# A written hand-over with the next weights cast earlier, and another order of the seven block products

## The chip, the cores and the metric

The kernel runs on one core of a Trainium2 chip. The core has a matrix engine (TensorE, PE in the rows; its weight loads are PEld), a vector engine (VectorE, DVE), a scalar engine (ScalarE, ACT), GpSimd (POOL) and a queue engine that issues transfers (SyncE, SP). Each engine works through its own list of instructions in order and waits where an operand or a buffer is not there yet. The metric is the device time of one execution in microseconds, the median of three runs.

## The reference

Two layers act on a sequence of 512 tokens with 1024 channels, all in float32. Each layer has three sublayers, each between two RMS norms and added to the residual `x`:

```
h = rms_norm(x, norm_pre[l, 0])
x = x + 0.5 * rms_norm(swiglu_ffn(h, ...ffn1...), norm_post[l, 0])
h = rms_norm(x, norm_pre[l, 1])
x = x + rms_norm(hybrid_mixer(h, ...), norm_post[l, 1])
h = rms_norm(x, norm_pre[l, 2])
x = x + 0.5 * rms_norm(swiglu_ffn(h, ...ffn2...), norm_post[l, 2])

def swiglu_ffn(h, w_gate, w_up, w_down):
    return (silu(h @ w_gate) * (h @ w_up)) @ w_down      # 1024 -> 2816 -> 1024
```

The mixer projects h into the inputs of three branches (stick-breaking attention, a gated convolution, gated linear attention), gates and sums them, and ends in an output projection of 1024 x 1024.

## The kernel before

**Products.** A float32 value is split into two parts, hi (a cast by ACT) and lo (the difference, by DVE), and each product is three matmuls: hi by hi, hi by lo and lo by hi. Every weight tile therefore costs a load into a `raw` buffer (half of one of three), one ACT cast `whi` and one DVE subtraction `wlo`. `whi` and `wlo` have five buffers each; a buffer is free again when the last matmul that reads it is done.

**Tokens.** The 512 tokens are four tiles of 128, numbered 0 to 3 (a, b, c, d in `out_proj`). A sublayer ends in `out_proj`: the last four weight tiles (`TAIL`) are kept back and multiplied token by token (`token(i)`), so that token 0's result is complete first. Token 3 goes tile by tile instead, so that each weight buffer comes free after six matmuls.

**Hand-over.** A `Hand` object per token holds what lies between the result and the next sublayer: `sum` (the block products of the FFN added up; nothing after a mixer), `square` (ACT, with a sum along the row), `mean` (one small DVE operation and a power on POOL), `scaled` (tn, the result by the post norm's weight), `add` (the new residual x, two DVE operations, and its two squares on ACT) and `normal` (hn, two DVE operations). `arrival(i, hns, forms)` transposes a token's hn on PE (eight transposes, tile pt), splits it into xh and xl, and, where the next sublayer is an FFN, hands it to `Forms.arrive`, which copies it to `xr` on ACT for tokens 0 and 1 and forms T1 to T4 on DVE for tokens 2 and 3. The copies are traced behind the split of the same PSUM banks.

The next sublayer's first weights are made by a generator `steps` of four steps, one `load_w` each: for an FFN two steps of the gate's and two of the up projection's first 256 columns, for a mixer four steps of two rows of blocks of V. The next stage's first matmuls are called pf (FFN; all eight k of the gate, then token i+1 arrives, then the up projection) or pv (mixer; token i+1 arrives after four of eight k). `second` is called at token 1's place there and ends token 3's hand-over.

**What fixes the order.** `pinned` chains an instruction behind the one that was traced just before it on the same engine. With `held[0]` true, the casts of `split` are pinned as well; else the planner of the framework may move them. All matmuls are pinned.

**Down projection.** `Down` multiplies 16 of the 22 row blocks as a 2 x 2 block product with seven products (`ORDER`: name, weight blocks, bank pair). Each has `PER` = 4 steps, and a step is twelve matmuls of 512 columns. Two of the other row blocks (`MIDDLE`) and four (`LAST`) are multiplied plainly; a middle step has 24 matmuls. `sums` loads the weights of a step and forms their sum (one DVE operation of 128 x 1024 for S3, S2, S1 and A22, none for A11, A12 and S4; S2 also adds two tiles of the hidden values first); S3 loads two blocks a step, the others one. `parts` makes the casts: dh and whi on ACT, dl and wlo on DVE. In A12 it also adds two tiles of the hidden values for S4. `ahead` runs `sums` of one step and `parts` of the step before it; it is called three times at the end of the block products of gate and up (`block_tiles`) and is four steps ahead of the matmuls (`AHEAD`). `tap` copies a bank pair to SBUF between products.

Of the kernel before, what the change touches and what calls it, by code (L numbers as in the profile page):

```python
# [41 lines left out]
def kernel(  # L42
# [184 lines left out]
    def arrival(i, hns, forms):  # L227

        t = slice(i * P, (i + 1) * P)
        if i == 0:  # L230
            room("xh")
            room("xl")
        pts = []
        for j, hn in enumerate(hns):
            pt = bank("pt")
            for k in range(4):
                transpose(pt[:, k * P:(k + 1) * P], hn[:, k * P:(k + 1) * P], ident)
            src = pt.rearrange("p (k t) -> p k t", t=P)
            split(cur["xh"][:, 4 * j:4 * j + 4, t], cur["xl"][:, 4 * j:4 * j + 4, t], src)
            pts.append(src)  # L240
        if forms is not None:
            forms.arrive(i, pts)
# [58 lines left out]
    def out_proj(w2d, nk, stat, tail, finish, upcoming, early, head=None):  # L301


        ld = lambda k: load_rows(w2d, k)
        fresh = head is None
        if fresh:
            banks = [[bank(f"o{i}{h}", "pb" if i < 3 else "pa") for h in range(2)] for i in range(NT)]
        else:
            banks, rest = head

        def mms(i, h, k, sh, sl, wh, wl):
            mm_out(banks[i][h], slice(i * P, (i + 1) * P), sh, sl, wh[:, HS[h]], wl[:, HS[h]],
                   fresh and k == 0, k == nk - 1)

        for k in range(nk - tail if fresh else 0):
            wh, wl = ld(k)
            sh, sl = stat(k)
            for i in range(NT):
                for h in range(2):
                    mms(i, h, k, sh, sl, wh, wl)  # L320
        if fresh:
            rest = [(k, ld(k), stat(k)) for k in range(nk - tail, nk)]
        def token(i):
            for h in range(2):
                for k, (wh, wl), (sh, sl) in rest:
                    mms(i, h, k, sh, sl, wh, wl)

        if early is None:
            for i in range(NT):
                token(i)  # L330
                finish(i, banks[i])
            return None

        held[0] = True
        a, b, c, d = [finish(i, banks[i]) for i in range(NT)]
        forms = finish(None, None)
        w, steps = early()
        next(steps)
        token(0)
        a.half(0)  # L340
        a.half(1)
        a.mean()
        token(1)
        a.add()
        b.half(0)
        a.mean()
        b.sum(1)
        a.normal()
        b.square(1)
        b.scaled(1)  # L350
        b.mean()
        token(2)
        c.half(0)
        b.add()
        c.half(1)
        b.mean()
        c.mean()
        b.normal()
        arrival(0, a.hns, forms)

        for k, (wh, wl), (sh, sl) in rest:
            for h in range(2):
                mms(NT - 1, h, k, sh, sl, wh, wl)
        c.add()
        next(steps)
        c.mean()
        d.sum(0)
        d.sum(1)
        d.square(0)
        d.square(1)  # L370
        next(steps)
        d.scaled(0)
        d.scaled(1)
        for _ in steps:
            pass
        d.mean()
        c.normal()
        held[0] = False

        def second():  # L380
            arrival(1, b.hns, forms)
            d.add()
            d.mean()
            d.normal()

        upcoming.extend((None, second, lambda: arrival(2, c.hns, forms), lambda: arrival(3, d.hns, forms)))
        return w

# [179 lines left out]
    class Down:  # L568
# [1 line left out]
        R1, R2 = slice(256, 512), slice(0, 256)  # L570
        PER = NP // 2

        ORDER = (("A11", ((0, 0),), "A"), ("S3", ((0, 1), (1, 1)), "C"), ("S2", ((0, 0),), "A"),
                 ("A12", ((1, 0),), "B"), ("S1", ((1, 1),), "A"), ("S4", ((1, 1),), "A"), ("A22", ((1, 0),), "C"))
        AHEAD = 4
        MIDDLE, LAST = (0, 1), (18, 19, 20, 21)

# [22 lines left out]

        def plan(self):

            self.steps = [(j, c) for j in range(5) for c in range(self.PER)]
            self.steps += [(None, f) for f in self.MIDDLE]
            self.steps += [(j, c) for j in (5, 6) for c in range(self.PER)]
            self.end = len(self.steps)
            self.steps += [(None, f) for f in self.LAST]

# [24 lines left out]
        def sums(self, p):  # L633

            self.load(p)
            j, c = self.steps[p]
            if j is None:
                return
            name, raws = self.ORDER[j][0], self.raw[p]
            tt = lambda o, a, b, op: pinned(nc.vector.tensor_tensor(o, a, b, op=op))  # L640
            kept = None if j == 0 else self.kept[:, 2 * c:2 * c + 2, :].rearrange("p k c -> p (k c)")
            src = raws[0]
            if name == "S3":
                tt(kept, raws[0], raws[1], ALU.subtract)
                src = kept
            if name == "S2":
                for q, x in enumerate(self.of(p)):
                    tt(x, self.s1[c][:, q], x, ALU.add)
                tt(kept, kept, raws[0], ALU.subtract)
                src = kept  # L650
            if name == "S1":
                pinned(nc.vector.scalar_tensor_tensor(src, kept, -1.0, raws[0], op0=ALU.mult, op1=ALU.subtract))
            if name == "A22":
                tt(src, kept, raws[0], ALU.add)
            self.raw[p] = src

        def parts(self, p):

            j, c = self.steps[p]
            sh, sl = (slot(x, F32R, "s") for x in ("dh", "dl"))  # L660
            hi, lo = (wp.tile([P, 1024], F32R, tag=t, name=t) for t in ("whi", "wlo"))
            of, src = self.of(p), self.raw.pop(p)
            n = 512 // len(of)
            cut = [slice(q * n, (q + 1) * n) for q in range(len(of))]
            for q, x in zip(cut, of):
                pinned(nc.scalar.copy(sh[:, q], x))
            pinned(nc.scalar.copy(hi, src))  # L667
            for q, x in zip(cut, of):
                pinned(nc.vector.tensor_tensor(sl[:, q], x, sh[:, q].bitcast(F32), op=ALU.subtract))
            pinned(nc.vector.tensor_tensor(lo, src, hi.bitcast(F32), op=ALU.subtract))  # L670
            if j is not None and self.ORDER[j][0] == "A12":
                for q, x in enumerate(of):
                    pinned(nc.vector.tensor_tensor(x, x, self.hid[self.F0 + 2 * c + q][:, self.R1], op=ALU.add))
            self.ready[p] = sh, sl, hi, lo

        def ahead(self):
# [10 lines left out]
        def product(self, p):  # L687
            j, c = self.steps[p]
            sh, sl, hi, lo = self.ready.pop(p)
            if j is None:  # L690
                for i, h in ((0, 1), (1, 1), (0, 0), (1, 0), (2, 0), (3, 0), (2, 1), (3, 1)):
                    mm_out(self.out[i][h], slice(i * P, (i + 1) * P), sh, sl, hi[:, HS[h]], lo[:, HS[h]],
                           st=(c == self.MIDDLE[0] and i < 2 and h == 1))
                return
            b = self.banks[self.ORDER[j][2]]
            for q in range(2):
                w = slice(q * 512, (q + 1) * 512)
                for i in range(2):
                    t = slice(q * 256 + i * P, q * 256 + (i + 1) * P)
                    mm_out(b[i], t, sh, sl, hi[:, w], lo[:, w], st=(q == 0 and c == 0 and j in (0, 1, 3)))  # L700

        def run(self, late):
            c0, d0, c1, d1, b0, b1 = (bank(n) for n in ("oC", "oD", "oC", "oD", "oB", "oB"))
# [12 lines left out]
            for p in range(self.end):  # L716
                j, c = self.steps[p]
                self.product(p)
                self.ahead()
                if c != self.PER - 1:  # L720
                    continue
                if j == 0:
                    tap(p1, "A")
                if j == 1:
                    tap(p7, "C")
                if j == 2:
                    tap(self.u2, "A")
                    late()
                if j == 4:
                    tap(self.u4, "A")  # L730
                    for i in range(2):
                        pinned(nc.vector.tensor_tensor(self.u4[i], p7[i], self.u4[i], op=ALU.subtract))

                    self.p1 = [slot("p1") for i in range(2)]
                    for i in range(2):
                        pinned(nc.scalar.copy(self.p1[i], p1[i]))
# [707 lines left out]
```

## Time and profile before

| | |
|---|---|
| median of three runs | 2360.44 us (2359.89 to 2360.69) |
| the profiled execution | 2361.5 us |
| its span, first to last instruction | 2359.8 us |
| PE busy | 2318.9 us, 98% |
| DVE busy | 1850.6 us, 78% |
| ACT busy | 1219.3 us, 52% |
| mean granted clock of PE | 0.997 |

The span is what the trace covers; the profiled execution's own time is 1.7 us longer, and 1.1 us above the median. A busy share is an average over all stages: with PE at 98%, the idle time is some 41 us, and it has to be looked for in the stage where it lies.

### The profile page before, as it was taken

The numbers are of one execution on the slowest core, as the hardware profiler recorded it, in microseconds if no ns is written. First come the engines' busy times: TensorE is split into PE (matmuls) and PEld (weight loads), VectorE is DVE, ScalarE is ACT, GpSimd is POOL, SyncE is SP. The second block draws the span as 40 slices with busy tenths as digits, with TensorE's granted clock in tenths as the row PEclk, the third lists the DMA queues.
The fourth block names the chain that finished last, engine by engine and source line by source line (L and its number), as shares of the span: only waits on it lengthen the run. The fifth ranks groups of instructions, "written<-read, shape, count | busy, mean of one in ns | idle before, by whom it ended". The sixth has DMA issues, their size and how long they took to land.

```text
span 2359.8 us, 36148 instructions
## 1 busy us (share of the span) xinstructions
PE 2318.9 (98%) x14072; PEld 2063.6 (87%) x14072; DVE 1850.6 (78%) x2755; ACT 1219.3 (52%) x2370; POOL 165.8 (7%) x277
## 2 busy tenths in 40 slices
PE   8999999999999999999999999999999999999998
PEld 7999887887888889998889998778878888999977
DVE  7888986859965378889778889778599644888896
ACT  5565655644323255566555566456333333555663
POOL 0000001201011100000000000012010211000000
PEclk9999999999999999999999999999999999999999
DMA  5333644231333223336423336341413322333362
GB/s 171 93 105 108 220 155 111 61 94 55 108 89 107 81 72 104 100 102 230 145 73 107 108 110 239 118 116 54 112 52 102 97 90 80 84 101 103 122 216 100
DMA packets 332763, 265.32 MB, mean 112 GB/s; under 512 B 12746, under 2 KB 285164, under 8 KB 332592
## 3 DMA queue, kind: packets, MB, share of 16 engines
q1 hardware_dynamic: 332592, 263.02, 36.9%
q8 instruction: 110, 1.80, 0.3%
q14 instruction: 61, 0.50, 0.1%
HBM read 260.88 MB, written 2.10 MB: 111 GB/s over the span
## 4 chain that ended last, share of the span: by engine, by line
PE 89%; DVE 6%; ACT 1%; DMA 1%; issue 1%; POOL 0%; SPq 0%; DVEq 0%; POOLq 0%; ACTq 0%
PE A L66 18%; PE gate L66 11%; PE C L66 9%; PE pb L66 6%; PE oA L66 5%; PE B L66 5%; PE pf L66 4%; PE o L66 3%; PE oC L66 3%; PE oB L66 3%; PE gr L66 2%; PE pa L66 2%; PE q L66 2%; PE gv L66 2%; PE pgl L66 2%; PE k L66 2%
## 5 line engine op out<-in xcount | busy, mean ns | idle before, releaser
L454 DVE TENSOR_TENSOR wlo<-raw,whi 128x1024 fp32r<-128x1024 f32 (+1 forms) x304 | 330.9, 1088 | 108.9 <-ACT whi L452 108.1
L452 ACT CAST whi<-raw 128x512 fp32r<-128x512 f32 x532 | 315.3, 620 | 159.9 <-DVE raw L454 159.9
L116 DVE TENSOR_TENSOR wlo<-raw,whi 128x1024 fp32r<-128x1024 f32 (+2 forms) x178 | 223.4, 1261 | 187.7 <-ACT whi L115 183.1
L115 ACT CAST whi<-raw 128x1024 fp32r<-128x1024 f32 (+2 forms) x178 | 185.1, 1044 | 353.3 <-PE gate L66 131.4
L454 DVE TENSOR_TENSOR raw<-raw 128x512 f32<-128x512 f32 x304 | 209.1, 688 | 5.8
L66 PE MATMUL A<-xh,whi 128*128 128x256 f32 x608 | 172.5, 284 | 0.0
L66 PE MATMUL A<-xh,wlo 128*128 128x256 f32 x608 | 172.0, 283 | 0.0
L66 PE MATMUL A<-xl,whi 128*128 128x256 f32 x608 | 172.0, 283 | 0.0
L1029 DVE SCALAR_TENSOR_TENSOR y<-u,cw,y 128x511 f32<-128x511 f32 (+14 forms) x240 | 166.6, 754 | 0.0
L667 ACT CAST whi<-raw 128x1024 fp32r<-128x1024 f32 x104 | 109.5, 1053 | 81.1 <-issue 36.3
L66 PE MATMUL gate<-xh,whi 128*128 128x512 f32 x384 | 151.3, 394 | 0.0
L66 PE MATMUL gate<-xh,wlo 128*128 128x512 f32 x384 | 149.8, 390 | 1.3 <-DVE wlo L116 1.3
L66 PE MATMUL gate<-xl,whi 128*128 128x512 f32 x384 | 149.6, 390 | 0.0
L670 DVE TENSOR_TENSOR wlo<-raw,whi 128x1024 fp32r<-128x1024 f32 x104 | 126.8, 1219 | 24.9 <-ACT whi L667 24.9
L268 POOL TENSOR_TENSOR rs<-ms,mhalf 128x1 f32<-128x1 f32 x44 | 25.9, 591 | 1464.5 <-DVE ms L266 1464.5
L66 PE MATMUL oA<-wlo,dh 128*128 128x512 f32 x304 | 119.6, 393 | 5.5 <-DVE wlo L670 5.5
L452 ACT COPY cp<-A 128x256 f32<-128x256 f32 x228 | 84.3, 370 | 70.9 <-PE A L66 69.9
L66 PE MATMUL oA<-whi,dl 128*128 128x512 f32 x304 | 118.4, 389 | 0.0
L66 PE MATMUL oA<-whi,dh 128*128 128x512 f32 x304 | 118.4, 389 | 0.0
L66 PEld LDWEIGHTS A<-xl,whi 128*128 128x128 f32 x608 | 116.5, 192 | 0.2
L66 PEld LDWEIGHTS A<-xh,whi 128*128 128x128 f32 x608 | 116.5, 192 | 0.2
L66 PEld LDWEIGHTS A<-xh,wlo 128*128 128x128 f32 x608 | 116.5, 192 | 0.0
(329 smaller groups left out, 7102.6 us busy)
## 6 DMA issues: line engine op xcount, KB each, us to landing
raw<-in_ffn_w_down_dram SPq DMA_DIRECT2D x152, 512.0 KB, 4.6
raw<-in_w_in_dram SPq DMA_DIRECT2D x108, 512.0 KB, 4.7
raw<-in_ffn_w_gate_dram SPq DMA_DIRECT2D x152, 256.0 KB, 3.4
raw<-in_ffn_w_up_dram SPq DMA_DIRECT2D x152, 256.0 KB, 4.5
raw<-in_w_branch_dram SPq DMA_DIRECT2D x24, 512.0 KB, 3.7
raw<-in_w_out_dram SPq DMA_DIRECT2D x16, 512.0 KB, 4.0
raw<-in_ffn_w_gate_dram SPq DMA_DIRECT2D x12, 512.0 KB, 4.8
raw<-in_ffn_w_up_dram SPq DMA_DIRECT2D x12, 512.0 KB, 4.6
```

The source lines that it names most:

```text
L66: tc.keep_in_program_order(nc.tensor.matmul(*a, **k))
L115: pin(nc.scalar.copy(hi, src))
L116: pin(nc.vector.tensor_tensor(lo, src, hi.bitcast(F32), op=ALU.subtract))
L268: nc.gpsimd.tensor_tensor(self.rs, ms, mhalf[:, 0:1], op=ALU.pow)
L452: copy = lambda o, i: pin(nc.scalar.copy(o, i))
L454: tt = lambda o, a, b, op: pin(nc.vector.tensor_tensor(o, a, b, op=op))
L667: pinned(nc.scalar.copy(hi, src))
L670: pinned(nc.vector.tensor_tensor(lo, src, hi.bitcast(F32), op=ALU.subtract))
L1029: nc.vector.scalar_tensor_tensor(y[:, back:], u[:, :S - back], cw[:, c, j:j + 1], y[:, back:], op0=ALU.mult, op1=ALU.add)
```

## The change

Two places are changed.

In `out_proj`, steps 2 to 4 of the next weights are cast right behind token 3's matmuls in the written order, with `b.normal()` (token 1) after step 2 and before steps 3 and 4. Before, step 2 stood behind `c.add()`, step 3 behind token 3's squares and step 4 behind its `scaled`; `b.normal()` stood ahead of token 0's arrival. Token 3's `square`, `scaled` and `mean` and token 2's second `mean` and `normal` go into `second`, behind token 1's arrival, whose casts are pinned now. `c.normal()` comes behind `d.mean()`, as before, and ahead of `d.scaled`. The last sublayer has no hand-over.

In `Down`, the order A11, S3, S2, A12, S1, middle, S4, A22 becomes A12, A11, S3, S2, A22, S1, middle, S4. The two additions to the hidden values that S4 needs move from `parts` of A12 to `sums` of S4. The taps and the load of the norms' weights (`late`) stay behind the same products. The number of matmuls, casts, sums and transfers is the same.

```diff
--- before.py
+++ after.py
@@ -355,30 +355,31 @@
         c.half(1)
         b.mean()
         c.mean()
-        b.normal()
         arrival(0, a.hns, forms)
 
         for k, (wh, wl), (sh, sl) in rest:
             for h in range(2):
                 mms(NT - 1, h, k, sh, sl, wh, wl)
+        next(steps)
+        b.normal()
+        for _ in steps:
+            pass
         c.add()
-        next(steps)
-        c.mean()
         d.sum(0)
         d.sum(1)
-        d.square(0)
-        d.square(1)
-        next(steps)
-        d.scaled(0)
-        d.scaled(1)
-        for _ in steps:
-            pass
-        d.mean()
-        c.normal()
         held[0] = False
 
         def second():
+            held[0] = True
             arrival(1, b.hns, forms)
+            held[0] = False
+            d.square(0)
+            d.square(1)
+            c.mean()
+            d.mean()
+            c.normal()
+            d.scaled(0)
+            d.scaled(1)
             d.add()
             d.mean()
             d.normal()
@@ -570,8 +571,8 @@
         R1, R2 = slice(256, 512), slice(0, 256)
         PER = NP // 2
 
-        ORDER = (("A11", ((0, 0),), "A"), ("S3", ((0, 1), (1, 1)), "C"), ("S2", ((0, 0),), "A"),
-                 ("A12", ((1, 0),), "B"), ("S1", ((1, 1),), "A"), ("S4", ((1, 1),), "A"), ("A22", ((1, 0),), "C"))
+        ORDER = (("A12", ((1, 0),), "B"), ("A11", ((0, 0),), "A"), ("S3", ((0, 1), (1, 1)), "C"),
+                 ("S2", ((0, 0),), "A"), ("A22", ((1, 0),), "C"), ("S1", ((1, 1),), "A"), ("S4", ((1, 1),), "A"))
         AHEAD = 4
         MIDDLE, LAST = (0, 1), (18, 19, 20, 21)
 
@@ -600,9 +601,9 @@
 
         def plan(self):
 
-            self.steps = [(j, c) for j in range(5) for c in range(self.PER)]
+            self.steps = [(j, c) for j in range(6) for c in range(self.PER)]
             self.steps += [(None, f) for f in self.MIDDLE]
-            self.steps += [(j, c) for j in (5, 6) for c in range(self.PER)]
+            self.steps += [(6, c) for c in range(self.PER)]
             self.end = len(self.steps)
             self.steps += [(None, f) for f in self.LAST]
 
@@ -638,7 +639,7 @@
                 return
             name, raws = self.ORDER[j][0], self.raw[p]
             tt = lambda o, a, b, op: pinned(nc.vector.tensor_tensor(o, a, b, op=op))
-            kept = None if j == 0 else self.kept[:, 2 * c:2 * c + 2, :].rearrange("p k c -> p (k c)")
+            kept = None if j < 2 else self.kept[:, 2 * c:2 * c + 2, :].rearrange("p k c -> p (k c)")
             src = raws[0]
             if name == "S3":
                 tt(kept, raws[0], raws[1], ALU.subtract)
@@ -648,6 +649,9 @@
                     tt(x, self.s1[c][:, q], x, ALU.add)
                 tt(kept, kept, raws[0], ALU.subtract)
                 src = kept
+            if name == "S4":
+                for q, x in enumerate(self.of(p)):
+                    tt(x, x, self.hid[self.F0 + 2 * c + q][:, self.R1], ALU.add)
             if name == "S1":
                 pinned(nc.vector.scalar_tensor_tensor(src, kept, -1.0, raws[0], op0=ALU.mult, op1=ALU.subtract))
             if name == "A22":
@@ -668,9 +672,6 @@
             for q, x in zip(cut, of):
                 pinned(nc.vector.tensor_tensor(sl[:, q], x, sh[:, q].bitcast(F32), op=ALU.subtract))
             pinned(nc.vector.tensor_tensor(lo, src, hi.bitcast(F32), op=ALU.subtract))
-            if j is not None and self.ORDER[j][0] == "A12":
-                for q, x in enumerate(of):
-                    pinned(nc.vector.tensor_tensor(x, x, self.hid[self.F0 + 2 * c + q][:, self.R1], op=ALU.add))
             self.ready[p] = sh, sl, hi, lo
 
         def ahead(self):
@@ -697,7 +698,7 @@
                 w = slice(q * 512, (q + 1) * 512)
                 for i in range(2):
                     t = slice(q * 256 + i * P, q * 256 + (i + 1) * P)
-                    mm_out(b[i], t, sh, sl, hi[:, w], lo[:, w], st=(q == 0 and c == 0 and j in (0, 1, 3)))
+                    mm_out(b[i], t, sh, sl, hi[:, w], lo[:, w], st=(q == 0 and c == 0 and j < 3))
 
         def run(self, late):
             c0, d0, c1, d1, b0, b1 = (bank(n) for n in ("oC", "oD", "oC", "oD", "oB", "oB"))
@@ -719,14 +720,14 @@
                 self.ahead()
                 if c != self.PER - 1:
                     continue
-                if j == 0:
+                if j == 1:
                     tap(p1, "A")
-                if j == 1:
+                if j == 2:
                     tap(p7, "C")
-                if j == 2:
+                if j == 3:
                     tap(self.u2, "A")
                     late()
-                if j == 4:
+                if j == 5:
                     tap(self.u4, "A")
                     for i in range(2):
                         pinned(nc.vector.tensor_tensor(self.u4[i], p7[i], self.u4[i], op=ALU.subtract))
```

## Rows read from the trace of the kernel before

**Rows 1.** Page, part 1: busy time, share of the span, instructions.
```profile
PE 2318.9 (98%) x14072; PEld 2063.6 (87%) x14072; DVE 1850.6 (78%) x2755; ACT 1219.3 (52%) x2370; POOL 165.8 (7%) x277
```

**Rows 2.** Five windows, one for each hand-over: busy time and count of each engine, clock, DMA.
```profile
356.25:387.12 30.87, 27.53 (x122) 21.34 (x120) 20.54 (x33) 16.46 (x31) 2.02 (x3) 0.94 0.37 105
835.21:864.91 29.70, 26.64 (x217) 25.83 (x216) 25.61 (x48) 18.38 (x34) 2.02 (x3) 1.00 0.27 72
1180.85:1213.00 32.15, 29.26 (x218) 28.32 (x217) 26.19 (x49) 16.87 (x33) 2.02 (x3) 0.89 0.24 67
1527.59:1558.78 31.19, 26.28 (x122) 20.12 (x120) 20.80 (x33) 16.48 (x31) 2.02 (x3) 1.00 0.37 103
2006.84:2036.82 29.98, 27.71 (x217) 27.31 (x216) 25.62 (x48) 18.16 (x34) 2.02 (x3) 0.94 0.26 71
```

**Rows 3.** Chain that ended last, in order of time: start, length, what.
```profile
378.14 0.87 PE pt L71 x8
379.01 8.18 PE pv L66 x36
...
856.45 8.63 PE pf L66 x72
```

**Rows 4.** Timeline of PE, H1: start, length, instruction, idle time before and its releaser.
```profile
350.71 0.48 PE L66 MATMUL oB<-whi,dh 128*128 128x512 f32 x1
...
359.17 0.50 PE L66 MATMUL pv<-whi,xh 128*128 128x512 f32 x1 [1.40 <-ACT whi L115]
```

**Rows 5.** Timeline of DVE, H1.
```profile
353.34 1.41 DVE L290 SCALAR_TENSOR_TENSOR hn<-x,rs,g 128x512 f32<-128x512 f32 x2 [0.61 <-POOL rs L268]
354.67 1.28 DVE L116 TENSOR_TENSOR xl<-pt,xh 128x512 fp32r<-128x512 f32 x2
355.87 1.40 DVE L282 SCALAR_TENSOR_TENSOR x<-tn,rs,x 128x512 f32<-128x512 f32 x2
359.15 1.23 DVE L116 TENSOR_TENSOR wlo<-raw,whi 128x1024 fp32r<-128x1024 f32 x1 [1.88 <-ACT whi L115]
...
360.42 0.68 DVE L747 TENSOR_TENSOR p<-oB,p 128x512 f32<-128x512 f32 x1
```

**Rows 6.** Timeline of ACT, H1.
```profile
351.66 1.07 ACT L115 CAST xh<-pt 128x512 fp32r<-128x512 f32 x2
...
357.46 0.63 ACT L261 ACTIVATE junk<-x 128x512 bf16<-128x512 f32 x1
...
358.09 1.03 ACT L115 CAST whi<-raw 128x1024 fp32r<-128x1024 f32 x1
```

**Rows 7.** A window right after H1's wait, columns as in rows 2.
```profile
359.20:362.70 3.50, 2.74 (x6) 1.89 (x7) 1.90 (x3) 1.48 (x5) 0.55 (x1) 0.67 0.28 71
```

**Rows 8.** Waits of PE and of its weight loads: us in total, times, longest.
```profile
PE oA L66 <- DVE wlo L670: 5.5, 10, 0.6
...
PEld oA L66 <- DVE wlo L670: 10.0, 11, 1.0
```

**Rows 9.** Timeline of the DMA queue on SP, before H1.
```profile
322.57 6.32 SPq L127 DMA_DIRECT2D raw<-in_w_in_dram  x4
```

**Rows 10.** Chain that ended last, front of the first down projection.
```profile
249.96 6.31 DMA raw<-in_ffn_w_down_dram
```

**Rows 11.** Timeline of ACT, H3 and H2.
```profile
1179.99 1.19 ACT L408 COPY xr<-pt 128x512 f32<-128x512 f32 x2 [2.66 <-DVE xl L116]
...
843.25 1.28 ACT L786 ACT_TABLE_LOAD   x1
```

**Rows 12.** Timeline of DVE, down projection of the first FFN.
```profile
270.08 0.76 DVE L640 TENSOR_TENSOR hid<-S,hid 128x256 f32<-128x256 f32 x2
270.75 1.22 DVE L640 TENSOR_TENSOR xh<-xh,raw 128x1024 f32<-128x1024 f32 x1
...
273.69 0.75 DVE L669 TENSOR_TENSOR dl<-hid,dh 128x256 fp32r<-128x256 f32 x2
...
275.50 0.75 DVE L669 TENSOR_TENSOR dl<-hid,dh 128x256 fp32r<-128x256 f32 x2
```

## Prediction

> **What bounds the kernel now.** I read the page's head and engine shares first: TensorE (PE) is busy 98% of the span [rows 1], so only the places where it stands still can be won. The list of what PE waited for names few of them, and two kinds lie in the change: the first tokens of a stage that follow a hand-over, and the front of the down projection. I then took one window per hand-over, from the first matmul of the new stage (pf or pv) to the first matmul after its four tokens [rows 2]. I call them H1 (FFN to mixer, layer 0), H2 (mixer to FFN), H3 (FFN to FFN), H4 (FFN to mixer, layer 1) and H5 (mixer to FFN). An undisturbed stretch gives the ideal: 36 pv matmuls in 8.18 us are 0.227 us each, 72 pf matmuls in 8.63 us are 0.120 us, eight transposes are 0.87 us [rows 3]. A mixer window holds 96 matmuls and three sets of transposes, 21.8 + 2.6 = 24.4 us; an FFN window 192 and three, 23.0 + 2.6 = 25.6 us. So H1 loses 30.9 - 24.4 = 6.5 us, H4 6.8, H2 4.1, H3 6.5, H5 4.4, together 28.3 us, 1.2% of the run.
>
> The timeline of H1 says why. PE does six pv matmuls with the pair of tiles cast first, then stands until 359.17 for whi on ScalarE (ACT) and on for wlo on VectorE (DVE) [rows 4]. ACT cast that tile only at 358.09, because the squares of token 2's new residual stood ahead of it, and they waited for x on DVE [rows 5, 6]. The clock comes on top: between 359.2 and 362.7 the granted clock is 0.67 of full [rows 7], a mix of the levels 2.4 and 1.2 GHz, right after that wait. H1, H3 and H5 have 0.94, 0.89 and 0.94 in their windows, H2 and H4 1.00 [rows 2]. A window of 32.15 us at 0.89 held 7.1 us of half clock, which cost H3 about 3.5 us.
>
> In the down projection PE waited for DVE's wlo: 5.5 us in ten places by the matmuls and 10.0 us by their weight loads [rows 8], over four FFNs. Matmul ends are modelled, so the truth lies between; I take 7.8.
>
> **The change, part by part.** *Casts ahead.* No matmul, cast or DMA is added. With T the first matmul of the new stage (356.25 in H1), token 3's 24 matmuls begin at 350.71 [rows 4] and go through the four last weight tiles in turn, six matmuls or 1.36 us each. The three casts need those tiles' buffers, which come free at about T-4.1, T-2.7 and T-1.4. ACT is free from T-3.5 (both xh casts end at 352.73 [rows 6]), so the three whi end at about T-2.5, T-1.4 and T-0.2: the buffers delay them hardly, and behind them on ACT stand only the squares of token 2, which are not ready yet. Their raw tiles are there: in H1 the four loads go out from 322.57 on within 6.32 us [rows 9], ahead of the last weight tiles' products, and a load takes some 6 us [rows 10].
>
> DVE now does, from T-3.5: xl of token 0 (1.3), wlo (1.2), hn of token 1 (1.4), wlo, wlo (2.4), x of token 2 (1.4), p (0.7) [rows 5], which fills it until T+4.9. PE wants the first new wlo at T+1.4 (it is there at T-1.0), token 1's hn at T+2.7 (there at T+0.4), the last two wlo at T+3.6 and T+5.0 (there at T+1.6 and T+2.8). What comes late next is token 1's xh and xl: x of token 2 is complete at T+4.2, its second square (0.63) ends at T+4.9, two xh casts (1.07) at T+6.0, so the first xl is there at about T+6.0 and the second at T+6.7; PE wants the first at 5.44 + 0.87 = T+6.3 and the second 2.7 us later. That is just in time. Token 2's hn (1.4) stands behind token 3's mean, whose two squares end at about T+7.5, so it is complete at T+9.0, wanted at T+9.0 (its second half half a us later). Token 3 then needs tn, x and hn (1.4 each) and two short waits for squares and the mean, an estimate of T+15, wanted at T+15.4. So H1 and H4 keep perhaps 0.3 us each: a gain of 6.2 + 6.5 = 12.7 us. No gain at all is the upper bound, 13.3 the lower.
>
> *FFN targets.* Here ACT also copies xr out of the same PSUM banks, and each copy starts only after DVE's xl has read its bank (1179.99 in H3, 2.66 us idle, released by xl [rows 11]). The first new cast is chained behind both copies. So whi ends at T-0.6 instead of T-2.5, and everything behind it on DVE is 1.7 us later: wlo at T+0.6, hn T+2.0 (wanted T+2.7, fine), the two wlo by T+4.4 (wanted T+3.6 for the first, there at T+3.2), x T+5.7, p T+6.3, first xh at T+7.1, first xl T+7.8: PE waits 1.3 us. Then xr of token 1 (1.19) and two squares of token 3 (0.63 each and reading their sums) push token 2's hn to T+11.4 and T+12.1, where PE wants it at T+10.3: 1.4 us more. That leaves H3 2.7 of its 6.5. After a mixer an activation-table load of 1.28 us [rows 11] must also find a place on ACT; I add half of it in H2 and H5, so 3.3 each of 4.1 and 4.4. Gain 3.8 + 0.8 + 1.1 = 5.7; bounds -1 (table load and a clock drop in each) and 12.
>
> About the clock the rows show a drop right behind H1's wait [rows 4, 7]. The Trainium skill, "TensorE: Matmul & The Clock Gate", section "What's actually happening", has the array's clock fall to half after idling and return after sustained work. By that rule the two waits that I leave in an FFN hand-over could each cost a drop as in H3; this is a rival below. The rows fit the rule in H1 and H3 but H4, with longer waits, kept 1.00.
>
> *Order of the seven products.* Per step PE does 12 matmuls of 512 columns, 2.72 us. DVE's step costs, start to start: S2 has two adds, a weight sum, two dl and wlo, 270.08 to 273.69 or 3.61 us; a step without adds or sum 273.69 to 275.50 or 1.81 us; the adds alone 0.67 us (270.08 to 270.75) [rows 12]. So S3, A22 and S1 cost 2.94 and A11 1.81, A12 with its adds 2.48. Before: A11 earns 4 x 0.91 = 3.6 us of lead, S3 and S2 use 4 x 0.22 + 4 x 0.89 = 4.4, and a load that lands 6.31 us after issue [rows 10] holds up S3: about 2 us of waiting per FFN, which is the 7.8 above. After: A12 (its adds go to S4, behind the two long middle steps, where DVE has time) and A11 earn up to 7.3 us, capped by five weight buffers to about 6; S3, S2, A22 and S1 then run 16 steps in a row at 49.7 us of DVE against 43.5 of PE, 6.2 short. Lead and shortage nearly cancel. I leave 0.7 us per FFN, 2.8 in all: gain 5.0. The bounds are everything gone (7.8) and no lead at all (24.8 instead of 7.8, a loss of 17); the value lies near the first, because eight steps with one load each come ahead of S3's two loads a step. Where the lead is short, the price falls into A22 and S1, and the middle steps end it.
>
> The sum: 12.7 + 5.7 + 5.0 = 23.4 us. The profiled execution took 2361.5 us (span 2359.8), the median is 2360.4, 1.1 lower; so 2361.5 - 23.4 - 1.1 = 2337.0 us.
>
> **Rivals.** *Waits move.* The chain on DVE behind the three casts (x, xl, hn) becomes what PE waits for at tokens 1, 2 and 3. For: it meets T+6.3, T+9.0 and T+15.4 with less than half a us in hand, and unpinned work (v splits, sides) may slip in. Against: DVE idles 1.88 us in H1 today, ahead of one wlo [rows 5]. If half the hand-over gain is eaten, 9 us go: 2346; if all, only the 5.0 remain: 2355.
>
> *Clock.* Each FFN hand-over drops to half clock for as long as H3 did: 3 x 3.5 = 10.5 us, 2347.5. For: 0.89 in H3; against: 1.00 in H2.
>
> *Slower.* The planner places unpinned DVE work ahead of the pinned chain: two wlo of the following weights (2.4 us) and, in the FFN, the forms. PE then waits some 2.7 us at token 1, 3 us at token 3, and half clock adds about 3: 8.7 per hand-over against 28.3/5 = 5.7 now. Five times 3.0 is 15 lost, less the 5.0: 2370. It decides when more than two such instructions stand in that stretch in every hand-over. Against: the code issues that work behind the pinned chain.
>
> *Down order backfires.* S3's loads land late, no lead: 17 us lost, 18.4 won, no change in sum: 2359. For: the load in the chain [rows 10]; against: the easier start.
>
> **How the numbers follow.** Forecast 0.60, waits move 0.18, clock 0.07, down order 0.08, slower 0.07. The likeliest gives 2337, with a range of its own of 2327 to 2345. Reaching to half of the second rival and the clock, 2327 to 2352 leaves out 2 in 10. A measurement tells 0.2%, 4.7 us, from no change. Faster takes the forecast, the clock and nearly all of "waits move": 0.84; same 0.09; slower 0.07.
>
> **What would show it.** After: H1 and H4 windows near 25 us at clock 1.00 with all whi before T; H3 near 28.4; waits of pv for whi gone; FFN waits at token 1 for xh or xl and at token 2 for hn of 1 to 1.5 us; PE's waits for wlo of oA below 3 us, in A22 or S1 and not in S2. The prediction is wrong if pv or pf matmuls of token 1 to 3 wait over 2 us in the mixer, if A22 and S1 stall by several us, or if time appears elsewhere in the mixer, where DVE would become late.

## The result: 28.7 us faster, and the profile after

The changed kernel takes 2331.43 us (median of four runs, 2329.28 to 2332.48), the kernel before 2360.16 beside it on the same chip: a ratio of 0.9877, interval 0.9860 to 0.9894. It is faster and inside the forecast range, 5.6 us below the forecast time of 2337.0. The profiled span is 2329.2 us, 30.6 below that of before; 1.9 us of this come from which executions were profiled (2361.5 before, 1.3 above the median beside it; 2330.92 now, 0.5 below its median). One execution of e11, the profiled one, was a disturbed one of 3045.6 us at a granted clock of 0.70, so it counts in no time and its windows are not read.

First the page's busy times, to be held against [rows 1].

```profile
PE 2307.6 (99%) x14072; PEld 2057.9 (88%) x14072; DVE 1848.9 (79%) x2755; ACT 1221.7 (52%) x2370; POOL 165.0 (7%) x277
```

The counts are those of before: nothing was added or removed. DVE and ACT do the same work. Of PE's 11.3 us less of busy time 8.9 lie in the five windows below; half clock is one cause, but not shown to be the only one, for H4, at 1.00 in both, fell too, from 26.28 to 24.53. Then the five hand-over windows, H1 to H5, with the columns and the bounds of [rows 2].

```profile
353.63:378.16 24.53, 24.53 (x121) 20.31 (x119) 19.94 (x33) 13.66 (x28) 1.62 (x3) 1.00 0.45 131
826.23:853.86 27.63, 26.52 (x217) 25.73 (x216) 25.04 (x48) 15.49 (x31) 2.02 (x3) 1.00 0.29 77
1167.82:1195.47 27.65, 26.48 (x217) 25.72 (x216) 25.60 (x49) 14.31 (x30) 2.02 (x3) 1.00 0.27 77
1508.91:1533.44 24.53, 24.53 (x121) 20.31 (x119) 20.20 (x33) 13.68 (x28) 1.62 (x3) 1.00 0.44 131
1981.54:2009.15 27.61, 26.50 (x217) 25.71 (x216) 25.03 (x48) 15.49 (x31) 2.02 (x3) 1.00 0.28 77
```

Against [rows 2] they gain 6.34, 2.08, 4.50, 6.66 and 2.36, in sum 153.89 - 131.95 = 21.9 us. In H1 and H4 PE's busy time equals the window: it never stands. The granted clock is 1.00 in all five. The drops of before (0.94, 0.89, 0.94) come to about 0.06 x 30.87 + 0.11 x 32.15 + 0.06 x 29.98 = 7.2 us, an estimate from rounded clocks, by which about a third of the windows' gain is clock given back and two thirds are waits.

The four down projections, from the first to the last of their 480 matmul starts, took 111.41, 112.23, 110.88 and 112.30 us before and take 109.52, 110.20, 109.72 and 109.37 now: 1.9 + 2.0 + 1.2 + 2.9 = 8.0 us. 21.9 + 8.0 is 29.9 of the span's 30.6. The other 0.7 us stand ahead of the first down projection (it starts at 243.88 instead of 244.61), where no line was changed; in the experiments that start lies anywhere between 243.3 and 244.6.

How much of these times was loss can be worked out too. An undisturbed step of twelve matmuls takes 2.72 us, so 480 starts span 108.6 us, and in the first three down projections token 0's eight transposes lie among them (0.9 us more). The rest is waiting: 1.9, 2.7, 1.4 and 3.7 us before, in sum 9.7, and 0.0, 0.7, 0.2 and 0.8 us now, in sum 1.7.

The timeline of DVE in H1, from T - 3.6 (T = 353.63, the first pv matmul), answers [rows 5]:

```profile
350.04 1.27 DVE L116 TENSOR_TENSOR xl<-pt,xh 128x512 fp32r<-128x512 f32 x2
351.24 1.21 DVE L116 TENSOR_TENSOR wlo<-raw,whi 128x1024 fp32r<-128x1024 f32 x1
352.37 1.40 DVE L290 SCALAR_TENSOR_TENSOR hn<-x,rs,g 128x512 f32<-128x512 f32 x2
353.70 2.35 DVE L116 TENSOR_TENSOR wlo<-raw,whi 128x1024 fp32r<-128x1024 f32 x2
355.97 1.41 DVE L282 SCALAR_TENSOR_TENSOR x<-tn,rs,x 128x512 f32<-128x512 f32 x2
357.29 0.68 DVE L748 TENSOR_TENSOR p<-oB,p 128x512 f32<-128x512 f32 x1
357.89 1.21 DVE L116 TENSOR_TENSOR wlo<-raw,whi 128x1024 fp32r<-128x1024 f32 x1
359.02 1.28 DVE L116 TENSOR_TENSOR xl<-pt,xh 128x512 fp32r<-128x512 f32 x2
```

No idle time stands in it. The order up to p is the one that the prediction wrote down. Then, at 357.89, a fourth wlo slips in between p and token 1's xl: it belongs to the weights after these, and its line is not pinned. That is the step of the rival "waits move"; it takes 1.21 us on DVE, and PE did not wait for it here (its window has no loss). The timeline of ACT answers [rows 6]:

```profile
350.00 2.17 ACT L115 CAST whi<-raw 128x1024 fp32r<-128x1024 f32 x2
352.47 1.06 ACT L115 CAST whi<-raw 128x1024 fp32r<-128x1024 f32 x1 [0.30 <-PE oA L66]
```

All three casts end by 353.53, ahead of T; only the third waited for its buffer, 0.30 us for an oA matmul. The lists of what PE and then its weight loads waited for answer [rows 8]:

```profile
PE pf L66 <- ACT xh L115: 2.1, 3, 1.7
PE pt L71 <- DVE hn L290: 1.9, 3, 0.7
PE pf L66 <- DVE xl L116: 1.5, 4, 0.6
...
PEld oA L66 <- DVE wlo L674: 2.0, 8, 0.3
```

No line of either list has pv. Of oA's 5.5 us of waiting by the matmuls no line is left, and of 10.0 by the weight loads 2.0. What remains are the FFN hand-overs: xl and xh at token 1, hn at token 2 (1.7 of xh's 2.1 us are one wait at the start of the kernel, at 11.35). In H3 (T = 1167.82), the timeline of PE shows the two places:

```profile
1174.32 0.28 PE L66 MATMUL pf<-whi,xl 128*128 128x256 f32 x1
1174.65 0.39 PE L66 MATMUL pf<-whi,xh 128*128 128x256 f32 x1
1174.87 0.28 PE L66 MATMUL pf<-wlo,xh 128*128 128x256 f32 x1
1175.60 0.39 PE L66 MATMUL pf<-whi,xl 128*128 128x256 f32 x1 [0.45 <-DVE xl L116]
1175.82 0.28 PE L66 MATMUL pf<-whi,xh 128*128 128x256 f32 x1
...
1178.20 0.28 PE L66 MATMUL pf<-whi,xl 128*128 128x256 f32 x1
1179.16 1.23 PE L71 MATMUL pt<-ident,hn 128*128 128x128 f32 x8 [0.68 <-DVE hn L290]
1180.14 0.36 PE L66 MATMUL pf<-whi,xh 128*128 128x256 f32 x1
```

Undisturbed, pf starts are 0.12 us apart [rows 3]. From 1174.32 to 1175.82 are four of them, 0.48, and 1.50 us went by: 1.0 lost at token 1. The transposes come 0.84 after the next slot, and the first matmul behind them 0.98 after their start instead of 0.80 (1170.69 to 1171.49 at token 1): 1.0 lost at token 2. Together that is the 2.0 us by which H3 stands above 25.6.

### The profile page after: what moved, and what is told of

Same layout as the page of the kernel before. It is cut to its first block, busy times and chain, and to the rows that moved or that the text cites. A ratio compares the mean times of both kernels' runs of the same rounds, so it can differ in the third digit from the quotient of the medians.

```text
span 2329.2 us, 36177 instructions
## 1 busy us (share of the span) xinstructions
PE 2307.6 (99%) x14072; PEld 2057.9 (88%) x14072; DVE 1848.9 (79%) x2755; ACT 1221.7 (52%) x2370; POOL 165.0 (7%) x277
## 4 chain that ended last, share of the span: by engine, by line
PE 97%; DVE 1%; ACT 1%; issue 0%; DMA 0%; SPq 0%; DVEq 0%; POOLq 0%; ACTq 0%
PE A L66 19%; PE gate L66 11%; PE C L66 9%; PE oA L66 9%; PE pb L66 6%; PE oC L66 5%; PE B L66 5%; PE o L66 3%; PE oB L66 3%; PE pf L66 3%; PE gr L66 2%; PE pa L66 2%; PE q L66 2%; PE gv L66 2%; PE pv L66 2%; PE pgl L66 2%
```

## The experiments

All medians are in us; the kernel before took 2360.35 to 2361.27 beside them, and the changed kernel again (e10) 2331.65.

**e1 and e2: each part alone.** e1 keeps the new hand-over and takes the old order of products, e2 the reverse. The core of what is in e1 and not in e2:

```diff
-        b.normal()
         arrival(0, a.hns, forms)
...
+        next(steps)
+        b.normal()
+        for _ in steps:
+            pass
         c.add()
...
         def second():
+            held[0] = True
             arrival(1, b.hns, forms)
+            held[0] = False
+            d.square(0)
...
```

> The hand-over of the changed kernel with the down projection of the kernel before. Theory (two separate gains that add): the five hand-over windows are those of the changed kernel, 24.5, 27.6, 27.7, 24.5 and 27.6 us, and the down projections keep their waits for wlo, so it gains 21.9 us: 2338 us. Rival (the earlier casts pull loads and DVE work about, and the order of the products is what lets them pay): windows of over 26 us for the mixer, a gain below 15 us, 2345 or more.

> The new order of the products with the hand-over of the kernel before. Theory: the hand-over windows stay at 30 to 32 us, PE's waits for wlo of oA fall from 5.5 us to nearly nothing, and it gains the other 8 us: 2352 us. Rival (the down projection gained only because the shorter hand-over shifted the loads): 2358 or more, with wlo waits of several us left.

e1 took 2339.37 (ratio 0.9911, 0.9896 to 0.9926), e2 2353.71 (0.9974, 0.9963 to 0.9985). The sums of the five windows, e1 and then e2, and PE's wait in e1's down projections:

```profile
sum 132.16, PE 128.60 PEld 117.83 DVE 115.84 ACT 72.65 POOL 9.32; mean PE 25.72 PEld 23.57 DVE 23.17 ACT 14.53 POOL 1.86
```

```profile
sum 154.02, PE 139.09 PEld 124.09 DVE 118.86 ACT 86.79 POOL 10.12; mean PE 27.82 PEld 24.82 DVE 23.77 ACT 17.36 POOL 2.02
```

```profile
PE oA L66 <- DVE wlo L671: 6.2, 11, 0.6
```

Each part does its own work in its own place: e1 has the windows of the changed kernel (131.95) and the wlo wait of before, e2 the windows of before (153.89) and no PE line for wlo in oA. Their gains, 21.0 and 6.6, add to 27.6 of the 28.7 to 29.1 that both give; the two hardly help or hinder each other.

**e3: the two adds alone.** The kernel before, with only the pair of adds moved from the parts of A12 to the sums of S4.

```diff
+            if name == "S4":
+                for q, x in enumerate(self.of(p)):
+                    tt(x, x, self.hid[self.F0 + 2 * c + q][:, self.R1], ALU.add)
...
-            if j is not None and self.ORDER[j][0] == "A12":
-                for q, x in enumerate(of):
-                    pinned(nc.vector.tensor_tensor(x, x, self.hid[self.F0 + 2 * c + q][:, self.R1], op=ALU.add))
```

> The kernel before, with nothing changed but the two additions for S4, which move from the casts of A12 to the sums of S4; the order of the products stays. Theory (the lead that DVE has when S3 begins sets the waits): the waits lie in S2, ahead of A12, and stay; 2360 us within 0.1%, PE's waits for wlo of oA still 5 to 6 us. Rival (the additions were the load too many on DVE): the waits shrink by half or more, 2356 us or less.

2361.80, ratio 1.0005 (0.9996 to 1.0015), and the wait for wlo in oA is still there:

```profile
PE oA L66 <- DVE wlo L673: 5.9, 11, 0.6
```

Moved by themselves, the adds are worth nothing.

**e8: A12 late again.** The changed kernel with A12 back behind the middle, its adds still in S4.

```diff
-        ORDER = (("A12", ((1, 0),), "B"), ("A11", ((0, 0),), "A"), ("S3", ((0, 1), (1, 1)), "C"),
-                 ("S2", ((0, 0),), "A"), ("A22", ((1, 0),), "C"), ("S1", ((1, 1),), "A"), ("S4", ((1, 1),), "A"))
+        ORDER = (("A11", ((0, 0),), "A"), ("S3", ((0, 1), (1, 1)), "C"), ("S2", ((0, 0),), "A"),
+                 ("A22", ((1, 0),), "C"), ("A12", ((1, 0),), "B"), ("S1", ((1, 1),), "A"), ("S4", ((1, 1),), "A"))
...
```

> The changed kernel with the products in the order A11, S3, S2, A22, A12, S1, middle, S4: A12 comes after the costly products instead of before them, its additions stay with S4. Theory (cheap steps ahead of the costly ones are what counts): S2 waits as in the kernel before, about 2 us per FFN, and A22 adds 0.2 us a step behind it, so 2.5 to 3 us per FFN: 2342 us. Rival (what counts is that A22 and S1 no longer sit at the end): no waits, 2332 us.

2343.54, 0.9928 (0.9913 to 0.9943): 12 us above the changed kernel, 3.0 in each FFN. The weight loads' waits come back:

```profile
PEld oA L66 <- DVE wlo L674: 12.4, 15, 1.0
```

The lead is the time from the end of a step's wlo to the start of its product. At the first step it is 5.0 us in the kernel before, the changed one and e8 alike: the first casts are made while PE is still in the stage before. At S3's first step it is 3.0 to 3.1 us in the four FFNs of the kernel before, and 3.1 in e8; with A12 in front it is 5.4 to 6.3. The DVE and PE rows of the kernel before, first FFN (251.25 + 1.22 to 255.52):

```profile
251.25 1.22 DVE L670 TENSOR_TENSOR wlo<-xh,whi 128x1024 fp32r<-128x1024 f32 x1
...
255.52 0.39 PE L66 MATMUL oC<-whi,dh 128*128 128x512 f32 x1
```

An obvious rival is that S3, which loads two blocks a step, merely gets its loads in time when it comes later. The lists of what DVE waited for with its weight sums (xh in these rows), before and then after, say no; in e8 it is 5.6 us:

```profile
DVE xh L640 <- DMA raw<-in_ffn_w_down_dram: 5.4, 5, 2.7
```

```profile
DVE xh L641 <- DMA raw<-in_ffn_w_down_dram: 5.3, 8, 1.2
```

DVE waits for loads as long as it did. So the cause is the lead that DVE has when the steps begin in which it is slower than PE: four cheap steps more ahead of them leave 2.3 to 3.2 us more of it, and the late loads are paid from it as well.

**e5 and e12: the written distance.** The lead was capped "to about 6" in the prediction. e5 lets the code run three steps ahead instead of four, e12 two (and leaves out the first of the calls of `ahead` at the end of the stage).

```diff
-        AHEAD = 4
+        AHEAD = 3
```

> The changed kernel with the casts of the down projection three steps ahead of the matmuls instead of four. Theory (S3, S2, A22 and S1 use up a lead of DVE over PE, 6.3 us of it when S3 begins): the cap lowers the lead by one step of 2.7 us to about 3.6, 6.2 are wanted, so PE waits 2.6 us per FFN late in the run of sixteen steps, 10 us in all: 2342 us, with waits of oA and oC for wlo back. Rival (the wait was caused by S2 coming right behind S3 early in the stage, not by the lead): no such waits, 2331 to 2333 us.

> The changed kernel with two steps of the down projection cast ahead in the written order instead of four. Three ahead cost only 1.4 us, since the written distance binds ScalarE and VectorE only where a tap stands among the casts on ScalarE and waits for its product. With two, the casts of the third S3 step stand behind the tap of A11's bank, 265.7 us or later where its product ends at 265.7. Theory (the lead of VectorE is what pays): the lead falls to about 1.4 us there, S2 and the products behind it want 3.6 + 1.9 us, so PE waits 2 to 5 us per FFN: 2346 us (2340 to 2352). Rival (the lead is not what pays): 2335 us or less.

e5 took 2333.07 (0.9884, 0.9869 to 0.9898), 1.4 us more than e10, with runs that overlap, where 10 had been expected: a miss. DVE's lead at the first step of S3 is 5.3 to 6.2 us there, nearly that of the changed kernel (5.4 to 6.3). e12 took 2342.86 (0.9922, 0.9907 to 0.9937), 11.2 above e10 and within the expected 2340 to 2352; its lead at S3's first step is 4.0 to 4.6 us and gone by the start of S2. The weight loads' waits, e5 and then e12:

```profile
PEld oA L66 <- DVE wlo L674: 3.9, 12, 0.9
```

```profile
PEld oA L66 <- DVE wlo L674: 12.2, 24, 1.0
```

and the timeline of ACT in e12, at the end of A11:

```profile
265.40 1.27 ACT L713 COPY xl<-oA 128x512 f32<-128x512 f32 x2 [4.73 <-PE oA L66]
```

Three steps ahead are nearly as good as four; at two the lead is too short, and one more thing shows. The tap, which copies A11's finished banks, stands in ACT's queue ahead of the casts of S3's third step and waits 4.73 us for A11's last matmul; the casts come behind it, and the lead is 1.8 us at that step.

**e4 and e7: which half of the hand-over.** The change moves the casts forward, and it moves seven steps of tokens 2 and 3 behind token 1's arrival. e4 puts those seven back ahead of the arrival and leaves the casts early; e7 leaves the arrival first and casts late, behind token 1's hn and token 2's x.

```diff
         d.sum(1)
+        d.square(0)
+        d.square(1)
+        c.mean()
+        d.mean()
+        c.normal()
+        d.scaled(0)
+        d.scaled(1)
         held[0] = False
...
```

```diff
-        next(steps)
         b.normal()
+        c.add()
         for _ in steps:
             pass
-        c.add()
         d.sum(0)
```

> The changed kernel, but with token 3's squares, means and scaled and token 2's normal written ahead of token 1's arrival, as in the kernel before; the three casts stay where the change puts them. Theory (the casts ahead pay only because token 1's arrival is served next): xl of token 1 comes behind about 3 us more of DVE work (two means, two tn, two hn), PE waits some 3 us at token 1 in each hand-over, less 0.7 where it waited for token 2's hn: windows of 27 to 28 us (mixer) and 30 (FFN), 13 us slower than the changed kernel: 2344 us, more if the clock falls. Rival (the casts ahead are all that matters): windows within 1 us of the changed kernel's, 2331 to 2335 us.

> The changed kernel with all three casts behind token 2's new residual and squares, and token 1's normal ahead of it, as in the kernel before; token 1's arrival stays ahead of token 3's work. Theory (both halves of the hand-over are needed): whi comes 3 us later than the first matmuls that want it, PE waits 2.7 to 3 us ahead of it once per hand-over and hardly later: windows of 27.3 (mixer) and 29 to 30 us (FFN), 13 us slower than the changed kernel: 2344 us. Rival (putting token 1's arrival first is what pays, the casts' place is free): windows within 1 us of the changed kernel's, below 2336 us.

e4 took 2353.99 (0.9974, 0.9964 to 0.9984), 10 us more than expected, e7 2338.48 (0.9911, 0.9895 to 0.9928), 6 less. Three of e4's windows (H1, H2, H4), the sum over all five, and its longest waits:

```profile
353.04:380.53 27.49, 25.13 (x122) 20.17 (x120) 20.09 (x33) 13.66 (x28) 2.07 (x3) 1.00 0.41 117
828.62:861.49 32.87, 28.82 (x218) 28.41 (x217) 26.88 (x50) 16.60 (x32) 2.02 (x3) 0.90 0.25 65
...
1521.33:1550.69 29.36, 26.73 (x121) 21.33 (x119) 20.44 (x33) 13.66 (x28) 2.07 (x3) 0.94 0.39 110
...
sum 152.99, PE 135.89 PEld 124.30 DVE 121.52 ACT 75.56 POOL 10.23; mean PE 27.18 PEld 24.86 DVE 24.30 ACT 15.11 POOL 2.05
```

```profile
PE pf L66 <- DVE xl L116: 7.8, 4, 2.4
PE pf L66 <- ACT xh L115: 6.4, 4, 1.7
```

and e7's sum:

```profile
sum 139.94, PE 132.02 PEld 120.50 DVE 112.06 ACT 82.68 POOL 11.82; mean PE 26.40 PEld 24.10 DVE 22.41 ACT 16.54 POOL 2.36
```

With early casts but token 1 behind (e4) the windows sum to 152.99, 0.9 us below 153.89, and the medians show no gain at all: e2, with the whole old hand-over, took 2353.71. The wait for whi is gone, and one for token 1's xl and xh has taken its place, with the clock down to 0.90 in H2. With the arrival first and late casts (e7) they sum to 139.94: 14.0 won (15.2 by the medians, from e2), and early casts add the other 8.0 (6.8, to e10), of which some 3.5 are clock by the estimate used above, for e7's H2 and H4 have 0.94. So the part that the change is named after is worth little by itself; it pays only because token 1 is then served first. (Neither is purely one half: e4 keeps token 1's hn behind the second step, and e7's casts are less late than before, where other work of tokens 2 and 3 stood ahead of them as well. How the 14.0 would divide then was not run.)

**e6, e9 and e11: what is left in the FFN.** The prediction blamed the copies of xr on ACT. e6 writes those of token 0 behind the three casts, and those of token 1 behind token 3's squares. e9 is e6 with `c.normal()` ahead of `d.mean()`; e11 is e6 with token 2's arrival pinned ahead of `d.normal()`.

```diff
-        arrival(0, a.hns, forms)
+        copies0 = arrival(0, a.hns, forms, copies=False)
...
         for _ in steps:
             pass
+        copies0()
...
-            arrival(1, b.hns, forms)
+            copies1 = arrival(1, b.hns, forms, copies=False)
             held[0] = False
             d.square(0)
             d.square(1)
+            copies1()
```

> The changed kernel with the copies xr of tokens 0 and 1 written behind the three casts and behind token 3's squares, so that neither the casts nor the squares are chained behind them. Theory (what is left in the FFN windows comes from these copies): the waits of pf for xh and xl of token 1 and for token 2's normal go, the three FFN windows fall from 27.6 to 26.2 us or a little above, mixer windows stay: 4 us faster than the changed kernel, 2327 us. Rival (what is left is the chain x, squares, xh on DVE and ACT, whatever the copies do): windows within 0.4 us of 27.6, 2331 us.

> As the kernel with the later copies, and token 2's normal written ahead of token 3's mean, so that it no longer waits for token 3's squares. Theory: token 2's normal was the next thing late by some tenths of a us in the FFN windows if at all, so it gains 0 to 1 us more: 2326 to 2327 us. Rival (token 3's chain is late then, since its mean comes later): windows grow by 0.5 us or more, 2329 us.

> The kernel with the later copies, and token 2's casts pinned ahead of token 3's normal, so that the second xl of token 2 no longer stands behind it on VectorE; token 2's forms come behind it. Theory (the 1.0 us still lost in the two windows after a mixer is this xl, behind which PE waits 0.75 us): both windows fall from 26.6 to 25.6 or 25.8 us, the others stay: 2 us faster than with the later copies, 2325 us. Rival (token 3's normal is late then, and the wait moves to token 3): windows of 26.5 us or more, 2327 us or more.

e6 took 2326.67 (2325.93 to 2328.38; 0.9857, 0.9843 to 0.9872), 5.0 below e10. Its windows H2 and H3, and what is left of H2 on PE and on DVE:

```profile
826.21:852.78 26.57, 25.86 (x218) 25.66 (x217) 24.43 (x47) 14.54 (x30) 2.02 (x3) 1.00 0.30 80
1167.28:1192.89 25.61, 25.61 (x217) 25.60 (x216) 24.59 (x48) 13.91 (x30) 1.62 (x3) 1.00 0.30 83
```

```profile
841.99 0.39 PE L66 MATMUL pf<-whi,xl 128*128 128x256 f32 x1 [0.70 <-DVE xl L116]
```

```profile
839.91 1.41 DVE L292 SCALAR_TENSOR_TENSOR hn<-x,rs,g 128x512 f32<-128x512 f32 x2 [0.40 <-POOL rs L270]
841.25 0.68 DVE L116 TENSOR_TENSOR xl<-pt,xh 128x512 fp32r<-128x512 f32 x1
```

H3 now stands at the ideal: PE is busy for all of its 25.61 us. So the copies held 2.0 us there, and 1.1 in H2 and 1.0 in H5. In those two, token 2's second xl still stands behind token 3's hn on DVE. e9 does not reach that, its longest wait for xl is still 0.7: 2328.21 (2327.19 to 2329.68), no difference from e6 that could be told. e11 does address it; its four other runs have a median of 2325.67 (2324.42 to 2327.01; 0.9851, 0.9835 to 0.9868), which cannot be told from e6 either; whether it removed the 0.70 us stays open, since no window of it can be read. The best kernel found is e6, or e11 beside it: about 2326, 5 us below the change.

## Why the prediction was right

The forecast was 23.4 us, and it was 28.7 by the medians. The terms below are read from the two profiled executions and add to 29.9:

- **Mixers**, 12.7 forecast, 6.34 + 6.66 = 13.0 measured. The order on DVE and the time of the three casts came out as worked out (third whi at T - 0.2 forecast, T - 0.1 in the trace); the 0.3 us left in each were not there.
- **FFN targets**, 5.7 forecast, 2.08 + 4.50 + 2.36 = 8.9 measured. The mechanism held: PE waits at token 1 for xh and xl and at token 2 for hn, and moving the xr copies (e6) removes it in H3. The sizes were off. At token 1 the forecast was 1.3 (its own times, T + 7.8 for the first xl and T + 6.3 for PE, are 1.5 apart) and the trace 1.0: the xl is there at T + 7.7, but PE comes to it only at T + 6.6, for the forecast took the mixer's 5.44 us for 24 matmuls, where the FFN's 48 take 5.76. At token 2 it was 1.4 and 1.0, with PE's place at T + 10.5 instead of T + 10.3. That is 0.7 us for each of three windows. The half table load, 0.64 in each of H2 and H5, cost nothing: those windows (27.63, 27.61) equal H3's (27.65), which has no such load.
- **Order of products**, 5.0 forecast, 8.0 measured. Both ends of this term were mis-sized: it took 7.8 us of waiting before, where the starts give 9.7 (the list of the weight loads, 10.0, was the nearer of its two), and left 2.8, where 1.7 are left. What is left lies in A22 and S1, as forecast, but not evenly: nothing in the first FFN, 0.7 and 0.8 in the second and fourth, where the lead at S3's first step was 5.6 and 5.4 us. In the first FFN it was 6.3: the wlo of S3's first step ends at 259.41 and its product begins at 265.67. The timelines of DVE and then of PE have that step and the third of S1:

```profile
258.19 1.22 DVE L674 TENSOR_TENSOR wlo<-xh,whi 128x1024 fp32r<-128x1024 f32 x1
...
302.52 1.22 DVE L674 TENSOR_TENSOR wlo<-raw,whi 128x1024 fp32r<-128x1024 f32 x1
```

```profile
265.67 0.39 PE L66 MATMUL oC<-whi,dh 128*128 128x512 f32 x1
...
303.75 0.39 PE L66 MATMUL oA<-whi,dh 128*128 128x512 f32 x1
```

From the one to the other PE took 38.08 us for 14 steps, 2.72 each: undisturbed. The lead fell from 6.3 us to 0.0, the wlo of 302.52 ending at 303.74. Of these 6.3 us 0.55 are a wait for a load; by the forecast's step costs the 14 steps use 5.8.

That the lead came to "about 6" is in part luck. The forecast has A12 and A11 earn it, capped by five weight buffers. In the trace of the first FFN 5.0 us are there at the first product (its wlo ends at 238.88, it begins at 243.88), A12's steps add nothing to it (4.4 at the fourth), and A11's take it to 7.1 at the third. ACT did wait for oB's matmuls twice in that stretch, 0.95 and 1.10 us, but DVE had no idle time of 0.1 us from 245.77 to 256.19, so buffers did not hold it there. It falls to 5.4 to 6.3 with S3's first sums and loads. And the reason that the value would lie near the good bound, "eight steps with one load each", did not hold: DVE waited as long for S3's loads as before, 5.3 against 5.4 us.

**The rivals.** "Waits move" had its mechanism (the unpinned wlo at 357.89) and not its price: in H3, where the same step stands at 1173.73, token 1's xl starts at 1174.87, 0.27 us after the xh that it needs. "Clock" did not come: waits of 0.45 to 0.7 us left the granted clock at 1.00 in all three FFN windows. The Trainium skill, "TensorE: Matmul & The Clock Gate", section "What's actually happening", has the clock fall to half after idling. The trace does not show that for waits as short as these; in e4, where they are longer, the clock was below 1.00 in four windows of five. "Slower" did not occur, and of "down order backfires" only the late loads did, paid by the lead. e4 shows how near the hand-over was to giving nothing: with token 1 behind it gains 0.9 us in the windows.

**What the prediction did not see** is that its first words, casts ahead, name the smaller half. Its own sums contain the larger one (token 1's xl at T + 6.0 because only x and two squares stand ahead of it), but it never asked what the casts would be worth with the old order of `second`.

## What to carry over

When a change removes the wait that a trace names, look up what is queued next on the same engine and price the change without the reordering too: here the windows gained 0.9 us with early casts and token 1 behind, and 21.9 with token 1 served first. A stretch in which one engine is slower than another can be paid for ahead by steps in which it is faster; sum both sides in us from start-to-start rows, late loads included: here a lead of 6.3 us cost nothing, one of 5.4 to 5.6 cost 0.7 to 0.8 us, and in e12 one of 4.0 to 4.6 cost 11 us over the four FFNs. And a copy that waits for another engine's reader holds up all that is queued behind it: moving it a few instructions back brought 5.0 us more.

## What the runs showed of the hardware

The same code and the same wait do not always cost the clock. In e4, H1 and H4 both have one wait of 2.21 us for token 1's xl (and 0.15 and 0.41 us for its xh); H1's granted clock is 1.00 and H4's 0.94, a mix of the two levels. From the timeline of PE, H1 and then H4:

```profile
362.63 0.50 PE L66 MATMUL pv<-whi,xl 128*128 128x512 f32 x1 [2.21 <-DVE xl L116]
```

```profile
1531.19 0.50 PE L66 MATMUL pv<-whi,xl 128*128 128x512 f32 x1 [2.21 <-DVE xl L116]
```

With the old hand-over unchanged, H4 had 1.00 in the kernel before [rows 2] and 0.89 in e2, behind first waits of 1.66 and 1.95 us for whi:

```profile
1522.14:1553.60 31.46, 28.68 (x122) 22.14 (x120) 20.82 (x33) 16.48 (x31) 2.03 (x3) 0.89 0.36 102
```

What decides it was not found. An xr copy that reads the PSUM bank of an xl starts only after that xl has ended (0.64 and 0.49 us idle in H3 after, 2.66 before [rows 11]); that this order comes from the program's semaphores and not from a port was not tried apart.
